# Four stages of a network kernel in another order: decay sums and levels, the out projection, grouped queries, the last rows

## The chip, the cores and the metric

The kernel runs on one core of a Trainium2 chip. The metric is the device time of one execution in microseconds (us). A core has five engines that work side by side: PE (TensorE: matmuls and transposes), DVE (VectorE), ACT (ScalarE), POOL (GpSimd) and SP, which issues most of the DMAs. Each takes its own instructions in order and waits on semaphores for the others. Matmul results land in PSUM, which this kernel uses as 8 banks of 128x512 float32; everything else lies in SBUF.

## The reference, cut to what matters

256 tokens of width 1024 go through a first block and a two-layer second block. In short:

```python
# first block, one layer
proj = rms_norm(x, l0_norm_mix) @ l0_w_in            # q (scaled), k, v, r, gate input
b = cumsum(log_sigmoid(gk_low @ w_gk_up + b_gk) / 16)
attn[i, j] = sum_k q[i, k] * k[j, k] * exp(b[i, k] - b[j, k])      # j <= i, 4 heads
x = x + (rms_norm(attn @ v) * silu(r)) @ l0_w_out
x = x + square(relu(rms_norm(x, l0_norm_ffn) @ l0_w_ff1)) @ l0_w_ff2
x = rms_norm(x, final_norm)
# second block, layer 0: neighbourhood attention and a gated feed-forward, latents and context
# second block, layer 1, latents only: grouped queries, 16 query heads on 4 key heads
q = axial_rope(rms_norm_2(q, q_gain));  k = axial_rope(rms_norm_2(k, k_gain))
s = einsum('bqhgd,bshd->bhgqs', q, concat([kc, k])) * dh ** -0.5
h = h + g1 * (softmax(s) @ concat([vc, v])) @ w_o
h = h + g2 * swiglu_ffn(ada_norm(h, norm_ffn[1]), ffn_w_in, ffn_w_out)
return rms_norm_2(h, norm_final_2)
```

## The kernel before, in words

**Precision and weights.** Every weight product is made of three passes (`mm3`, lines 177 to 180): weight and activation are each split into a rounded part and a remainder. A weight unit is a 128x1024 tile; `w_load` (L150) has SP load it into one of five raw buffers, `w_split` makes the rounded part on ACT (L161) and the remainder on DVE (L162). Both go into a pool of twelve buffers, so six units fit at most. `wnext` hands out the next unit of a fixed list, and `cap[0]` says how many units from the one handed out on are split ahead (3 means two more). For a token tile of 128, `mm_r` makes 6 matmuls of 128x512 (two halves of the output by three passes), `mm_h` 3.

**Order.** The tile framework plans the order on each engine from the program's order and from its own estimates of durations. Where `manual_schedule` is open, the named engines keep the order of the program: SP, ACT and DVE for the first products (lines 367 to 474), ACT alone until the gate products end (475 to 654), DVE and ACT at the very end (1509 to 1543). PE is planned everywhere.

**Decay sums and levels (lines 428 to 579).** Eight units give q and k, transposed (loop `f`). `decay_sums(t)` makes the cumulated log decay `bT` of a token tile: 4 matmuls (L431) and 2 ACT copies (L433); tile 0 at `f == 7`, tile 1 after the first unit (`k == 0`) of the next loop. That loop makes v from eight units; beside it `core_step` builds the 128x128 attention of both tiles by a diagonal, seven levels (distances 1 to 64) and the part across the tiles. The first part of a level makes subtractions on DVE (L501, L502), an exp on ACT (L504), products on DVE (L507, L508); its second part 16 small matmuls on PE (L522) and a masked copy on DVE (L528), for the two widest levels copies on ACT (L525, L516). `core_step` runs the second part of one unit and the first part of the next: one step of lead. `conditioning` (k == 2) starts loads of 1 MB, which wait for `bT` of tile 1.

**Out projection (lines 660 to 681).** Eight units of `l0_w_out`. Units 0 to 2 are multiplied with both token tiles at once; units 3 to 7 are kept (`late`), multiplied with tile 0, then with tile 1, so that `residual` of tile 0 (L658) and its transposes and splits (`to_T`: L217 on PE, L224 on ACT, L225 on DVE) lie beside the products of tile 1. `heads_T(range(4, 8))` (L630 on PE, L633, L634) stands after unit 2; all eight transposes of `to_T` stand before the last unit of tile 1.

**Grouped queries (lines 1245 to 1451).** Keys and values come first, `kv_finish` normalizes and rotates the keys and transposes them (L1237, L1241, L1243). Then the queries, in two halves of 8 heads by two token tiles, each of 8 steps of 3 matmuls. `q_proj(0)` makes half 0 for both tiles in turn, 16 steps, beside `kv_finish`; then a one-column Exp loads ACT's table (L1326); `q_finish` of half 0, tile 0 (L1274 to L1298) runs beside ten steps of half 1 (`q_proj1`). `staged` starts a head of a tile (`gqa_unit`) on each round: scores (L1387, L1388), maximum on DVE (L1393), exp on ACT (L1396), scaling (L1402 on DVE, L1400 on ACT), transposes (L1406), copies (L1413) and, for each four heads, the products with v (L1420). On each round `qfill` adds one of the six steps of half 1 that are left, steps of the other `q_finish` and of the out projection.

**Last rows (lines 1509 to 1543).** The last four units of the last down projection are kept back. For tile 1 three column pieces are made (512, 256, 256); each gets gate and residual (L1499, L1500) and its square sum on ACT (L1502). Then comes the root on POOL (L1538), ACT scales half 1 (L1539), DVE half 0 (L1541), and two DMAs write them.

Of the kernel before, what the change touches and what calls it, by code (L numbers as in the profile page):

```python
# [19 lines left out]
KD = D // P  # L20
# [63 lines left out]
def net(ctx, tc, x, xt, small, gk_up, gk_b, g_onorm, wst, final_norm, ctx_in, ctx_t, ada, ada_b, cvec,  # L84
# [122 lines left out]
    def to_T(*args):  # L207
        for _ in to_T_steps(*args):
            pass
# [226 lines left out]
    for f in range(8):  # L436
# [35 lines left out]
        if f == 7:  # L472
            decay_sums(0)
# [85 lines left out]


    vtok = []
    ac = [[bank() for _ in range(2)] for _ in range(NT)]
    for k in range(KD):
        u = wnext(("r", "w_in", k))
        for t in range(NT):
            mm_r(ac[t], u, xT[k], t, k == 0, k == KD - 1)
        if k == 0:
            decay_sums(1)
        if k == 2:
            conditioning()  # L570
        if k == 5:
            cap[0] = 3
        core_step()
# [88 lines left out]
    for k in range(KD):  # L662
        u = wnext(("r", "w_out", k))
        if k == 0:
            for t in range(NT):
                gated_heads(t, 1)
        if k < KD - 5:
            for t in range(NT):
                mm_r(ac[t], u, yT[k], t, k == 0, False)
        else:  # L670
            late.append((k, u))
    heads_T(range(4, KD))
    hT = new_T()
    for t in range(NT):
        for k, u in late:
            if (t, k) == (1, KD - 1):
                to_T([xin[0]], hT, 0, vc[:, V_FFN0, :])
            mm_r(ac[t], u, yT[k], t, False, k == KD - 1)
        residual(xin[t], ac[t])
    late.clear()  # L680
# [564 lines left out]
    def q_proj(hf, ac):  # L1245
        for kp in range(4):
            u = wnext(("h", "gqa_qkv", 2 * kp, 512 * hf))
            for j in range(2):
                k = 2 * kp + j
                for t in range(2):  # L1250
                    mm_h(ac[t], u, j, bT2[k], t, k == 0, k == KD - 1)
                    yield

    q1_units = []

    def q_proj1(ac, t):
        for kp in range(4):
            if t == 0:
                if kp == 2:
                    cap[0] = 0  # L1260
                q1_units.append(wnext(("h", "gqa_qkv", 2 * kp, 512)))
            for j in range(2):
                k = 2 * kp + j
                mm_h(ac[t], q1_units[kp], j, bT2[k], t, k == 0, k == KD - 1)
                yield
# [56 lines left out]
    aq = [bank(), bank()]  # L1322
    beside(q_proj(0, aq), back)
    run(back, 100)
    warm = col()
    A.activation(out=warm[:, 0:1], in_=aq[0][:, 0:1], func=AF.Exp, scale=0.0)  # L1326
    aq0, acq1 = [aq[0], t2([512])], aq[1]
    back = q_finish(0, aq0, 0)
    aq = [bank(), bank()]
    projs = [q_proj1(aq, t) for t in range(2)]  # L1330
    for n in range(10):
        run(projs[n // 8])
        run(back)
        if n == 1:
            A.copy(out=aq0[1], in_=acq1)
    run(back, 100)

    def finishes():

        yield from q_finish(1, aq, 0)  # L1340
        yield from q_finish(0, aq0, 1)
        run(projs[1], 9)
        q1_units.clear()
        yield from q_finish(1, aq, 1)
# [94 lines left out]
    def qfill(n):  # L1439
        run(projs[1])  # L1440
# [84 lines left out]
    ms, zs_ = col(), [t2([512]) for _ in range(2)]  # L1525
    for n, (hf, lo, w) in enumerate(((0, 0, 512), (1, 0, 256), (1, 256, 256))):
# [7 lines left out]
        if n > 0:  # L1534
            V.tensor_tensor(out=zs_[1][:, lo:lo + w], in0=zs_[1][:, lo:lo + w], in1=nfb[1][:, lo:lo + w], op=ALU.mult)
# [3 lines left out]
    A.activation(out=zs_[1], in_=zs_[1], func=AF.Copy, scale=r)  # L1539
    out_rows(nc.scalar, 1, 512, zs_[1])  # L1540
    V.scalar_tensor_tensor(out=zs_[0], in0=zs_[0], scalar=r, in1=nfb[0], op0=ALU.mult, op1=ALU.mult)  # L1541
    out_rows(nc.sync, 1, 0, zs_[0])
# [107 lines left out]
```

## Time and profile before

| what | value |
|---|---|
| time, median of 3 runs | 1268.24 us (1267.25 to 1268.48) |
| the profiled execution | 1267.33 us, of it the span of the profile 1265.5 us |
| PE busy | 1249.0 us, 99% of the span |
| DVE busy | 920.0 us, 73% |
| ACT busy | 686.1 us, 54% |
| granted PE clock | 0.998 |

The span runs from the first instruction to the last; 1.83 us of the time lie around it. A row of the timeline has start, length, engine, line, operation, tiles, and in brackets how long the engine was idle before it and what ended that. The records of matmuls overlap: one lasts longer than the time until the next one starts, so that PE's idle time is more than its rows show. PEld is the load of the stationary operand, in the shade of PE.

### The profile page before, as it was taken

The page shows a single profiled execution, that of the slowest core. Times are in us where ns is not written, and L with a number is a line of the kernel's source. Part 1 is how long each engine was busy: PE and PEld are TensorE (multiplying, and loading weights), DVE is VectorE, ACT ScalarE, POOL GpSimd, SP SyncE. Part 2 cuts the span into 40 slices and gives each one's busy share as a digit, 9 for nine tenths or more (in the row PEclk, how much of TensorE's full clock was granted, in tenths as well). Part 3 has the DMA queues.
Part 4 walks back from the last instruction along what each step waited for, and adds up shares of the span by engine and source line. Part 5 has one row for each costly group of instructions (what it writes and reads, how often), then busy time and mean ns, then how long its engine had stood idle before and what let it go on. Part 6 is the DMA issues. An engine that isn't in the chain of part 4 may idle for free.

```text
span 1265.5 us, 18648 instructions
## 1 busy us (share of the span) xinstructions
PE 1249.0 (99%) x6874; PEld 1043.6 (82%) x6874; DVE 920.0 (73%) x1629; ACT 686.1 (54%) x1335; POOL 79.2 (6%) x139
## 2 busy tenths in 40 slices
PE   9999999999999999999999999999999999999997
PEld 8878898988888777789888888888888677899996
DVE  5868788797988888777877667623668888655555
ACT  7565655666548888754332122323457797644443
POOL 1000000030100000001000000000002320000000
PEclk9999999999999999999999999999999999999999
DMA  8646587877572334463656777633664224665650
GB/s 302 202 133 212 190 293 255 283 267 260 183 251 98 126 114 114 155 197 114 210 184 204 248 258 252 219 100 102 198 200 117 67 84 128 215 190 184 187 180 34
DMA packets 68507, 231.22 MB, mean 183 GB/s; under 512 B 8048, under 2 KB 8736, under 8 KB 68416
## 3 DMA queue, kind: packets, MB, share of 16 engines
q1 hardware_dynamic: 68128, 229.68, 56.0%
q8 instruction: 54, 0.88, 0.3%
q10 hardware_dynamic: 288, 0.35, 0.1%
q14 instruction: 37, 0.30, 0.1%
HBM read 228.93 MB, written 1.07 MB: 182 GB/s over the span
## 4 chain that ended last, share of the span: by engine, by line
PE 84%; DVE 7%; ACT 6%; issue 1%; DMA 1%; POOL 0%; POOLq 0%; SPq 0%; DVEq 0%; ACTq 0%
PE b L178 26%; PE b L179 25%; PE b L180 25%; DVE wl L162 2%; PE b L1420 1%; ACT wh L161 1%; PE b L217 1%; PE b L1406 1%; PE b L522 1%; DMA raw<-in_wst_dram 1%; DVE a L309 1%; ACT t L878 1%; DVE t L309 1%; PE b L1387 0%; PE b L957 0%
## 5 line engine op out<-in xcount | busy, mean ns | idle before, releaser
L161 ACT CAST wh<-raw 128x1024 fp32r<-128x1024 f32 x310 | 322.8, 1044 | 391.2 <-PE b L179 295.7
L162 DVE TENSOR_TENSOR wl<-raw,wh 128x1024 fp32r<-128x1024 f32 x310 | 375.0, 1215 | 157.7 <-ACT wh L161 154.0
L179 PE MATMUL b<-t,wl 128*128 128x256 f32 (+1 forms) x1120 | 365.8, 327 | 0.3 <-DVE wl L162 0.3
L178 PE MATMUL b<-t,wh 128*128 128x256 f32 (+1 forms) x1120 | 366.1, 327 | 0.0
L180 PE MATMUL b<-t,wh 128*128 128x256 f32 (+1 forms) x1120 | 365.3, 327 | 0.0
L178 PE MATMUL b<-wh,t 128*128 128x512 f32 (+1 forms) x748 | 298.2, 401 | 1.2 <-ACT t L235 0.6
L180 PE MATMUL b<-wl,t 128*128 128x512 f32 (+1 forms) x748 | 295.1, 395 | 0.0
L179 PE MATMUL b<-wh,t 128*128 128x512 f32 (+1 forms) x748 | 294.9, 394 | 0.1
L179 PEld LDWEIGHTS b<-t,wl 128*128 128x128 f32 x1120 | 210.8, 188 | 22.6 <-DVE wl L162 0.6
L178 PEld LDWEIGHTS b<-t,wh 128*128 128x128 f32 x1120 | 210.7, 188 | 22.3 <-issue 0.2
L180 PEld LDWEIGHTS b<-t,wh 128*128 128x128 f32 x1120 | 210.5, 188 | 20.6 <-DVE t L236 0.2
L180 PEld LDWEIGHTS b<-wl,t 128*128 128x128 f32 x748 | 140.5, 188 | 33.7
L178 PEld LDWEIGHTS b<-wh,t 128*128 128x128 f32 x748 | 140.4, 188 | 32.6 <-ACT t L235 1.0
L179 PEld LDWEIGHTS b<-wh,t 128*128 128x128 f32 x748 | 140.8, 188 | 31.0 <-DVE t L634 0.6
L309 DVE CUSTOM_DVE_ANT_0 a<-a,crow 128x1024 f32<-128x1024 f32 x96 | 117.0, 1226 | 28.3 <-DMA a<-in_ada_dram 27.7
L309 DVE CUSTOM_DVE_ANT_0 t<-a,crow 128x1024 bf16<-128x1024 f32 x64 | 78.5, 1236 | 8.8 <-DMA a<-in_ada_dram 8.8
L1065 DVE TENSOR_TENSOR t<-b,t 128x512 f32<-128x512 f32 (+1 forms) x42 | 23.6, 563 | 59.4 <-PE b L180 52.2
L190 POOL TENSOR_TENSOR c<-c,mhalf 128x1 f32<-128x1 f32 x21 | 14.2, 674 | 537.7 <-DVE c L189 537.6
L324 POOL TENSOR_TENSOR mod<-mod,bcol 128x8 f32<-128x8 f32 x20 | 14.4, 719 | 478.3 <-DVE mod L309 476.0
L1071 ACT CAST t<-t 128x512 fp32r<-128x512 f32 (+1 forms) x42 | 21.7, 517 | 34.6 <-DVE t L1065 34.6
L197 ACT ACTIVATE t<-t 128x512 f32<-128x512 f32 x40 | 24.8, 624 | 10.8 <-DVE t L1034 6.4
L1396 ACT ACTIVATE t<-b,c,c 128x512 f32<-128x512 f32 x32 | 25.9, 811 | 3.4 <-POOL c L1394 3.4
(239 smaller groups left out, 1201.4 us busy)
## 6 DMA issues: line engine op xcount, KB each, us to landing
raw<-in_wst_dram SPq DMA_DIRECT2D x310, 512.0 KB, 4.4
a<-in_ada_dram SPq DMA_DIRECT2D x96, 512.0 KB, 4.4
t<-in_rpb_dram SPq DMA_DIRECT2D x16, 256.0 KB, 4.1
t<-row SPq DMA_DIRECT2D x12, 256.0 KB, 4.9
t<-in_ctx_dram SPq DMA_DIRECT2D x8, 256.0 KB, 5.8
t<-in_xt_dram SPq DMA_DIRECT2D x4, 256.0 KB, 5.9
t<-in_x_dram SPq DMA_DIRECT2D x4, 256.0 KB, 6.3
crow<-in_cvec_dram SPq DMA_DIRECT2D x2, 512.0 KB
```

The source lines that it names most:

```text
L161: A.copy(out=h[:, :n], in_=raw[:, :n])
L162: V.tensor_tensor(out=l[:, :n], in0=raw[:, :n], in1=h[:, :n], op=ALU.subtract)
L178: T.matmul(o, lhsT=lh, rhs=rh, start=first, stop=False)
L179: T.matmul(o, lhsT=ll, rhs=rh, start=False, stop=False)
L180: T.matmul(o, lhsT=lh, rhs=rl, start=False, stop=last)
L190: G.tensor_tensor(out=ms[:, 3:4], in0=ms[:, 2:3], in1=mhalf[:, 0:1], op=ALU.pow)
L197: A.activation(out=junk[hf], in_=halves[hf], func=AF.Square, scale=1.0 / 32.0, accum_out=ms[:, hf:hf + 1])
L309: V.tensor_tensor_reduce(out=raw if ci == n_c - 1 else t2([D], BF16), in0=raw, in1=crow[ci], scale=1.0, scalar=0.0, op0=ALU.mult, op1=ALU.add,
L324: G.tensor_tensor(out=m, in0=m, in1=bcol[:, L, v, :], op=ALU.add)
L1065: V.tensor_tensor(out=a, in0=pg_[:, :n], in1=a, op=ALU.mult)
L1071: A.copy(out=h, in_=a)
L1396: A.activation(out=pl, in_=sl, func=AF.Exp, scale=r, bias=mx[:, 1:2], accum_out=mx[:, 2:3])
```

## The change

Decay sums: tile 0 after `f == 6`, tile 1 after `f == 7`. Levels: two units (the diagonal, whose first part is empty, and the first level) are opened ahead of the loop, so that `core_step` opens a unit two steps before its matmuls. Out projection: four units are kept instead of five; the transposes of heads 4 and 5 stand after unit 1, those of 6 and 7 after unit 2; the steps of `to_T` for tile 0 stand 2, 3 and 3 ahead of the last three units of tile 1. Grouped queries: half 0 is made for tile 0 alone, then for tile 1 with its four units kept in SBUF; the table load and `q_finish` of tile 0 start after the first eight steps; only five steps of half 1 stand ahead of `staged`, and eleven are left for its rounds (two on each of the first two rounds, then one); `cap` is 2 there instead of 0. Last rows: the products with the final norm's gains go into tiles of their own, `ys_`, that of half 0 ahead of the root; the last operation on DVE becomes a scaling by one column.

```diff
@@ -469,8 +469,8 @@
         if f == 5:
             later_operands()
             cap[0] = 5
-        if f == 7:
-            decay_sums(0)
+        if f > 5:
+            decay_sums(f - 6)
     in_order.__exit__(None, None, None)
     in_order = tc.manual_schedule(engines={mybir.EngineType.Activation})
     in_order.__enter__()
@@ -557,6 +557,10 @@
             open_.append(core.pop(0))
             run(open_[-1])
 
+    for _ in range(2):
+        open_.append(core.pop(0))
+        run(open_[-1])
+
 
     vtok = []
     ac = [[bank() for _ in range(2)] for _ in range(NT)]
@@ -564,8 +568,6 @@
         u = wnext(("r", "w_in", k))
         for t in range(NT):
             mm_r(ac[t], u, xT[k], t, k == 0, k == KD - 1)
-        if k == 0:
-            decay_sums(1)
         if k == 2:
             conditioning()
         if k == 5:
@@ -664,19 +666,22 @@
         if k == 0:
             for t in range(NT):
                 gated_heads(t, 1)
-        if k < KD - 5:
+        if k < KD - 4:
             for t in range(NT):
                 mm_r(ac[t], u, yT[k], t, k == 0, False)
         else:
             late.append((k, u))
-    heads_T(range(4, KD))
+        if k in (1, 2):
+            heads_T((2 * k + 2, 2 * k + 3))
     hT = new_T()
+    first_T = to_T_steps([xin[0]], hT, 0, vc[:, V_FFN0, :])
     for t in range(NT):
         for k, u in late:
-            if (t, k) == (1, KD - 1):
-                to_T([xin[0]], hT, 0, vc[:, V_FFN0, :])
+            if t == 1 and k > KD - 4:
+                run(first_T, k - KD + 5)
             mm_r(ac[t], u, yT[k], t, False, k == KD - 1)
         residual(xin[t], ac[t])
+    run(first_T, KD)
     late.clear()
 
 
@@ -1242,26 +1247,14 @@
                 else:
                     V.tensor_copy(out=dst[h][:, pos:pos + P], in_=pt[:, h * P:(h + 1) * P])
 
-    def q_proj(hf, ac):
+    def q_proj(hf, t, units, o):
+
         for kp in range(4):
-            u = wnext(("h", "gqa_qkv", 2 * kp, 512 * hf))
+            if t == 0:
+                units.append(wnext(("h", "gqa_qkv", 2 * kp, 512 * hf)))
             for j in range(2):
                 k = 2 * kp + j
-                for t in range(2):
-                    mm_h(ac[t], u, j, bT2[k], t, k == 0, k == KD - 1)
-                    yield
-
-    q1_units = []
-
-    def q_proj1(ac, t):
-        for kp in range(4):
-            if t == 0:
-                if kp == 2:
-                    cap[0] = 0
-                q1_units.append(wnext(("h", "gqa_qkv", 2 * kp, 512)))
-            for j in range(2):
-                k = 2 * kp + j
-                mm_h(ac[t], q1_units[kp], j, bT2[k], t, k == 0, k == KD - 1)
+                mm_h(o, units[kp], j, bT2[k], t, k == 0, k == KD - 1)
                 yield
 
     qst, qf = {}, {}
@@ -1319,29 +1312,43 @@
     beside(kv_steps(acl), back)
     run(back, 100)
     back = alternate([kv_finish(acl, t) for t in range(2)])
-    aq = [bank(), bank()]
-    beside(q_proj(0, aq), back)
+    qu, aq = [[], []], [[bank(), None], [None, None]]
+    for _ in q_proj(0, 0, qu[0], aq[0][0]):
+        next(back, None)
+    warm = col()
+    A.activation(out=warm[:, 0:1], in_=aq[0][0][:, 0:1], func=AF.Exp, scale=0.0)
+    aq[0][1] = bank()
+    first = q_finish(0, aq[0], 0)
+    for _ in q_proj(0, 1, qu[0], aq[0][1]):
+        next(back, None)
+        next(first, None)
+    qu[0].clear()
+    q01 = t2([512])
+    A.copy(out=q01, in_=aq[0][1])
+    aq[0][1] = q01
+
+    def q1_products():
+        for t in range(2):
+            if t == 0:
+                cap[0] = 2
+            aq[1][t] = bank()
+            yield from q_proj(1, t, qu[1], aq[1][t])
+        qu[1].clear()
+
+    q1_ = q1_products()
+    for _ in range(5):
+        run(q1_)
+        next(back, None)
+        next(first, None)
     run(back, 100)
-    warm = col()
-    A.activation(out=warm[:, 0:1], in_=aq[0][:, 0:1], func=AF.Exp, scale=0.0)
-    aq0, acq1 = [aq[0], t2([512])], aq[1]
-    back = q_finish(0, aq0, 0)
-    aq = [bank(), bank()]
-    projs = [q_proj1(aq, t) for t in range(2)]
-    for n in range(10):
-        run(projs[n // 8])
-        run(back)
-        if n == 1:
-            A.copy(out=aq0[1], in_=acq1)
-    run(back, 100)
+    run(first, 100)
 
     def finishes():
 
-        yield from q_finish(1, aq, 0)
-        yield from q_finish(0, aq0, 1)
-        run(projs[1], 9)
-        q1_units.clear()
-        yield from q_finish(1, aq, 1)
+        yield from q_finish(1, aq[1], 0)
+        yield from q_finish(0, aq[0], 1)
+        run(q1_, 20)
+        yield from q_finish(1, aq[1], 1)
 
     def oproj():
 
@@ -1437,7 +1444,7 @@
     gorder = [(h, t) for t in range(2) for h in range(16)]
 
     def qfill(n):
-        run(projs[1])
+        run(q1_, 2 if n < 2 else 1)
         run(finish_, 0 if n < 3 else 2 if n < 8 or n % 4 == 0 else 1)
         run(oproj_)
 
@@ -1522,7 +1529,7 @@
         out_rows(nc.sync, 0, 512 * hf, z0[hf])
 
 
-    ms, zs_ = col(), [t2([512]) for _ in range(2)]
+    ms, zs_, ys_ = col(), [t2([512]) for _ in range(2)], [t2([512]) for _ in range(2)]
     for n, (hf, lo, w) in enumerate(((0, 0, 512), (1, 0, 256), (1, 256, 256))):
         o = bank()[:, 0:w] if n else ac[1][0]
         last_mms(o, 1, 512 * hf + lo, w, n > 0)
@@ -1531,15 +1538,15 @@
             V.scalar_tensor_tensor(out=ms[:, 3:4], in0=ms[:, 0:1], scalar=EPS, in1=ms[:, 1:2], op0=ALU.add, op1=ALU.add)
         else:
             first_rows(n)
-        if n > 0:
-            V.tensor_tensor(out=zs_[1][:, lo:lo + w], in0=zs_[1][:, lo:lo + w], in1=nfb[1][:, lo:lo + w], op=ALU.mult)
+        for y, z, g in ((ys_[1][:, lo:lo + w], zs_[1][:, lo:lo + w], nfb[1][:, lo:lo + w]), (ys_[0], zs_[0], nfb[0]))[:(0, 2, 1)[n]]:
+            V.tensor_tensor(out=y, in0=z, in1=g, op=ALU.mult)
     V.tensor_tensor(out=ms[:, 2:3], in0=ms[:, 2:3], in1=ms[:, 3:4], op=ALU.add)
     r = ms[:, 4:5]
     G.tensor_tensor(out=r, in0=ms[:, 2:3], in1=mhalf[:, 0:1], op=ALU.pow)
-    A.activation(out=zs_[1], in_=zs_[1], func=AF.Copy, scale=r)
-    out_rows(nc.scalar, 1, 512, zs_[1])
-    V.scalar_tensor_tensor(out=zs_[0], in0=zs_[0], scalar=r, in1=nfb[0], op0=ALU.mult, op1=ALU.mult)
-    out_rows(nc.sync, 1, 0, zs_[0])
+    A.activation(out=ys_[1], in_=ys_[1], func=AF.Copy, scale=r)
+    out_rows(nc.scalar, 1, 512, ys_[1])
+    V.tensor_scalar(out=ys_[0], in0=ys_[0], scalar1=r, scalar2=None, op0=ALU.mult)
+    out_rows(nc.sync, 1, 0, ys_[0])
     in_order.__exit__(None, None, None)
```

## The prediction

> **What bounds the kernel now.** I read the page first, then PE's list of waits, the windows, and the timeline where PE waits.
>
> ```profile
> span 1265.5 us, 18648 instructions
> PE 1249.0 (99%) x6874; PEld 1043.6 (82%) x6874; DVE 920.0 (73%) x1629; ACT 686.1 (54%) x1335; POOL 79.2 (6%) x139
> ```
> ```profile
> PE b L522 <- DVE t L508: 1.6, 1, 1.6
> ...
> PE b L1406 <- DVE t L1402: 1.1, 3, 0.5
> PE b L1406 <- DVE c L1398: 0.8, 2, 0.5
> ...
> PE b L217 <- DVE t L225: 0.4, 1, 0.4
> ...
> PE b L179 <- DVE wl L162: 0.3, 1, 0.3
> ```
>
> PE is busy for 99% of the span, and no edit takes a matmul away. So the change can only win what PE waits, or shorten the work after its last matmul. The listed waits are what it aims at: the levels (L522), the start of grouped queries (L1406), the out projection (L217, a weight at L179).
>
> A wait costs more than its row says:
>
> ```profile
> 969.42 0.39 PE L178 MATMUL b<-wh,t 128*128 128x512 f32 x1
> 969.65 0.39 PE L179 MATMUL b<-wh,t 128*128 128x512 f32 x1
> ```
> ```profile
> 112.97 0.48 PE L178 MATMUL b<-wh,t 128*128 128x512 f32 x1
> 113.30 0.40 PE L179 MATMUL b<-wh,t 128*128 128x512 f32 x1
> ```
>
> Matmuls start 0.23 us apart but are shown 0.39 long, so 0.16 of each wait lies under the record before it; I add 0.16 per wait. The second pair stands right behind a group of transposes: its gap is 0.33 instead of 0.23. So each change from transposes to weight products costs about 0.1, and an edit that breaks a group up pays that again.
>
> ```profile
> core 0: us, PE busy (x) PEld busy (x) DVE busy (x) ACT busy (x) POOL busy (x), PEclk, DMA share, GB/s
> 37.00:44.40 7.40, 7.40 (x46) 6.49 (x45) 3.70 (x4) 3.75 (x7) 0.42 (x3) 1.00 0.90 341
> 44.40:72.00 27.60, 26.05 (x156) 22.40 (x155) 27.19 (x64) 11.34 (x16) 0.00 (x0) 1.00 0.36 115
> 965.20:986.00 20.80, 20.80 (x105) 16.96 (x103) 16.29 (x41) 13.15 (x30) 5.35 (x6) 1.00 0.58 175
> 986.00:992.50 6.50, 6.24 (x30) 4.80 (x28) 4.68 (x9) 4.62 (x9) 2.63 (x4) 1.00 0.26 81
> 992.50:1006.40 13.90, 11.65 (x70) 7.53 (x70) 12.80 (x31) 12.23 (x33) 4.60 (x11) 1.00 0.14 39
> ```
>
> In two of these stretches DVE, not PE, sets the pace: 27.19 of 27.60 us in the levels, 12.80 of 13.90 where grouped queries start. The stretch ahead of each has DVE at 50% and 78%. Work that starts earlier fits in there.
>
> **Decay sums and levels.**
>
> ```profile
> 38.16 1.05 PE L431 MATMUL b<-cm,t 128*128 128x128 f32 x8
> ...
> 39.26 0.65 ACT L433 COPY t<-b 128x256 f32<-128x256 f32 x2 [1.38 <-PE b L431]
> ...
> 44.45 0.42 DVE L501 TENSOR_TENSOR t<-t 128x256 f32<-128x256 f32 x1
> ```
> ```profile
> 64.09 1.34 DVE L528 COPY_PREDICATED t<-masks,b 128x512 f32<-128x512 uint8 x2
> ...
> 71.28 2.02 PE L522 MATMUL b<-t 128*128 128x128 f32 x16 [1.55 <-DVE t L508]
> 71.39 0.42 DVE L508 TENSOR_TENSOR t<-t,t 128x256 f32<-128x256 f32 x1
> ```
>
> Six levels take DVE from 44.45 to 71.81, 27.4 us; PE catches up at the sixth and waits 1.55 + 0.16 = 1.71. In the new order L431 of tile 1 moves ahead of 12 products (12 x 0.23 = 2.8 us), and the first level opens at once instead of a step later: the copies of L433 end at 39.26 + 0.65 - 2.8 = 37.1, and DVE can begin. In front of the sixth level it then has the same 27.4, the 3.7 that it did from 37.0 to 44.4, and two pairs of masked copies less (L528, 2.7), since those of the fourth and fifth level now come behind: it ends at 37.1 + 27.4 + 3.7 - 2.7 = 65.5. PE asks for the sixth level one step (2.8) earlier, at 71.28 - 1.71 - 2.8 = 66.8. So the stall goes whole or down to a few tenths, against 1.71 now; PE has weight products left to plan in between. ACT keeps the program's order there, so the weight casts queue behind two exps that wait for DVE; `cap` 5 has four units split ahead, which covers it, and without that cover it costs the 1.7 us of four subtractions (4 x 0.42). The 1 MB that POOL releases from `bT` comes up to 2.8 us earlier into a window with the DMAs at 0.90; the same four units cover that, and at 341 GB/s its whole price would be 3 us. I take **-1.6**; ends 0 and -1.8.
>
> **Out projection.**
>
> ```profile
> 128.64 0.58 PE L217 MATMUL b<-cm,t 128*128 128x128 f32 x2 [0.37 <-DVE t L225]
> ```
>
> The eight transposes of tile 0 stand in one block and wait for their banks behind L225: 0.37 + 0.16. Spread by 2, 3 and 3 over products of 1.4 us (6 x 0.23) each, a group of three needs three L225 in that time, and the block's wait goes. The late weight (0.3 + 0.16) goes too: with four kept units instead of five, the last unit is asked for 6 matmuls, 1.4 us, later. Against it stand two more changes between transposes and products, 0.2. The transposes of heads 4 and 5 come a unit earlier and may wait for the gated heads; the plan has unit 2 to put in front. Sum 0.53 + 0.46 - 0.2 = 0.8, **-0.8**; ends +0.3 (nothing but the breaks) and -1.2.
>
> **Grouped queries.**
>
> ```profile
> 965.21 0.40 PE L178 MATMUL b<-wh,t 128*128 128x512 f32 x1
> ...
> 967.03 1.23 DVE L162 TENSOR_TENSOR wl<-raw,wh 128x1024 fp32r<-128x1024 f32 x1 [0.24 <-ACT wh L161]
> ...
> 976.88 0.39 PE L180 MATMUL b<-wl,t 128*128 128x512 f32 x1
> ```
> ```profile
> 986.17 0.50 PE L1387 MATMUL b<-t,t 128*128 128x512 f32 x1
> ...
> 992.72 0.63 PE L1406 MATMUL b<-cm,t 128*128 128x128 f32 x4 [0.47 <-DVE t L1402]
> ```
> ```profile
> 1006.39 0.50 PE L178 MATMUL b<-wh,t 128*128 128x512 f32 x1 [0.27 <-ACT t L1413]
> ```
>
> From 992.72 to 1006.39 PE has used up the six filler steps and waits seven times; the two rows are the first and the last of them. The windows give 0.26 + 2.25 = 2.5 us without PE, and with 7 x 0.16 it is 3.6. The change leaves five more steps, 15 matmuls, 5 x 0.70 = 3.5 us, for these rounds. The stall shrinks by that only if the rounds, DVE's pace included, also start 3.5 earlier, at 986.17 - 3.5 = 982.7. Two conditions. The first queries: half 0 of tile 0 ends 8 steps after 965.21, at 970.8, and before it took 986.17 - 976.88 = 9.3 from the last product of half 0 to the first score, so 980.1; met with 2.6 to spare, the table load moving along on ACT. DVE: its 16.29 + 4.68 + 12.80 = 33.8 us from 965.2 to 1006.4 must fit in 37.7, 90%, just under the 92% of the dense stretch. I take off five breaks of 0.1 and 0.2 for the tightness: **-2.8**; ends +1 (DVE late for the first scores by one split of 1.2, filler no help) and -3.6. The split of the out projection's first unit, which `cap` 2 moves ahead of the rounds, is in the 33.8 already.
>
> **Last rows.**
>
> ```profile
> 1257.30 0.28 PE L180 MATMUL b<-wl,t 128*128 128x256 f32 x1
> ```
> ```profile
> 1258.03 0.42 DVE L1535 TENSOR_TENSOR t<-t,t 128x256 f32<-128x256 f32 x1 [0.97 <-ACT t L1502]
> 1258.38 0.41 DVE L1499 TENSOR_TENSOR t<-b,t 128x256 f32<-128x256 f32 x1
> ...
> 1259.61 0.19 ACT L1502 ACTIVATION_READ_ACCUMULATOR t<-t 128x1 f32 x1
> 1259.83 0.42 DVE L1535 TENSOR_TENSOR t<-t,t 128x256 f32<-128x256 f32 x1 [0.51 <-ACT t L1502]
> 1260.17 0.15 DVE L1536 TENSOR_TENSOR c<-c 128x1 f32<-128x1 f32 x1
> ...
> 1261.04 0.72 ACT L1539 ACTIVATE t<-t,c 128x512 f32<-128x512 f32 x1 [1.25 <-POOL c L1538]
> ```
>
> L1535 writes in place and waits for ACT's square, 0.97 and 0.51. With `ys_` it needn't: the first begins at 1257.06, and the added product of 512 columns (two of 256, 0.7) follows; DVE is free at 1258.1, after PE's end, so L1499 gains 0.28. The second no longer stands in front of L1536, which then follows the accumulator's read, 1259.61 - 0.28 + 0.19 = 1259.52, at 1259.57 instead of 1260.17. DVE's last operation gets shorter, but ACT's 0.72 beside it ends last. **-0.6**; ends -0.3 and -0.9.
>
> **Sum:** 1.6 + 0.8 + 2.8 + 0.6 = 5.8. The profiled execution took 1267.33, so 1261.5; it lies 0.9 under the median of the runs, and from 1268.24 the forecast is **1262.4**.
>
> **A rule against it.** Granted PEclk is 1.00 even from 992.5 to 1006.4, where PE is busy for 11.65 of 13.90 us. The Trainium skill, Perfetto Trace Analysis, section Matmul Optimizations, says that the engine scales power with use, so "it's important that matmuls execute back-to-back in batches". By that rule, breaking up transposes and fillers could lower the clock. The row shows no such drop in a far looser stretch.
>
> **Rivals.** (1) DVE holds the start of grouped queries: for it speak 92% in the dense stretch, against it the 78% ahead of it. That term becomes 0 to -0.6: 1265.0. Chance 0.22. (2) The planner does not follow: PE's order is its own, and it hoisted filler before; out projection and queries then give nothing, 1268.24 - 2.2 = 1266.0. Chance 0.09. (3) Slower: a weight unit for one tile lasts only 6 matmuls, 1.40 us, and its split costs 1.04 on ACT and 1.22 on DVE.
>
> ```profile
> L161 ACT CAST wh<-raw 128x1024 fp32r<-128x1024 f32 x310 | 322.8, 1044 | 391.2 <-PE b L179 295.7
> L162 DVE TENSOR_TENSOR wl<-raw,wh 128x1024 fp32r<-128x1024 f32 x310 | 375.0, 1215 | 157.7 <-ACT wh L161 154.0
> ```
>
> If splits stop running ahead, because the kept units fill the twelve buffers, each of the eight takes 2.26 instead of 1.40: +6.9, and the queries' gain is lost: 1268.24 - 3.0 + 6.9 = 1272.1. It decides once a split ends more than 1.40 after the one before. Against it: the last split of half 0 ended at 968.3 and would be asked for at 965.21 + 3 x 1.40 = 969.4. Chance 0.07. (4) The clock: one of PE's loose stretches, such as the 13.9 us, if the clock fell by half there, would cost up to 13.9: 1276. Chance 0.01. (5) More is won, as later waits of the rounds move too: 1259. Chance 0.06.
>
> The forecast keeps 0.55. The range 1259.4 to 1266.8 leaves out (3), (4), part of (5) and the far ends of (1) and (2), under 0.2. A difference under 0.2%, 2.5 us, can't be told from none: the line lies at 1265.7. Faster: 0.55 + 0.06 + 0.16 of (1) + 0.03 of (2) = 0.80; slower 0.08; same 0.12.
>
> **What would show it.** Levels: no wait of L522 for L508, L501 from about 37. Out projection: no wait at L217. Queries: first score near 979 (982.7 less the gains before it), weight products between the first L1406 groups, DVE over 85% ahead of them. Last rows: no wait of the two products for L1502, the root 0.6 sooner after PE's end. Wrong if PE waits for L162 in the query halves, or if the L1406 waits still add to 2 us or more.

## The result and the profile after

The changed kernel takes 1260.24 us (median of 5 executions, 1259.76 to 1261.04); the kernel before took 1267.59 beside it (5 executions, 1267.24 to 1268.48). The ratio is 0.9943, with a 95% interval of 0.9929 to 0.9957: faster, by 7.35 us. The forecast was 1262.4, worked out from 1268.24; of the 2.2 us between, 0.65 is that the kernel before itself has a lower median with two more executions.

The profiled execution after took 1259.76, its span is 1258.0. Its page:

```profile
span 1258.0 us, 18656 instructions
PE 1246.1 (99%) x6874; PEld 1043.5 (83%) x6874; DVE 920.0 (73%) x1630; ACT 685.8 (55%) x1335; POOL 80.8 (6%) x139
```

PE does the same 6874 matmuls in a shorter span and DVE one instruction more. PE's list of waits, which was headed by L522:

```profile
PE b L121 <- POOL mhalf L137: 1.3, 1, 1.3
PE b L178 <- ACT t L235: 0.6, 1, 0.6
PE b L179 <- DVE wl L162: 0.5, 1, 0.5
PE b L1413 <- DVE t L1409: 0.4, 1, 0.4
...
PE b L1413 <- ACT t L1407: 0.4, 1, 0.4
```

L522 and L217 are gone. L1413, which was L1406, keeps two waits; the third row is still there and will matter below. (Against the kernel before, the lines of the changed kernel stand 5 higher from L669 on, 7 lower in `q_finish`, L1262 to L1292, and 7 higher from L1330 on.) The windows after, those of grouped queries cut at the same landmarks as before, in us, with busy time and number of PE, PEld, DVE, ACT and POOL, then PEclk, DMA share and GB/s:

```profile
37.00:44.40 7.40, 7.40 (x44) 6.40 (x44) 6.62 (x16) 4.20 (x6) 0.84 (x3) 1.00 0.87 331
44.40:70.00 25.60, 25.60 (x159) 22.59 (x158) 25.60 (x57) 11.33 (x16) 0.00 (x0) 1.00 0.38 114
961.57:978.90 17.33, 17.33 (x91) 14.25 (x90) 14.44 (x38) 12.13 (x30) 5.65 (x6) 1.00 0.44 146
978.90:985.40 6.50, 6.50 (x30) 5.22 (x29) 5.97 (x14) 4.35 (x8) 2.61 (x4) 1.00 0.56 164
985.40:999.64 14.24, 13.85 (x83) 10.00 (x81) 13.26 (x29) 12.96 (x33) 4.63 (x11) 1.00 0.27 75
```

DVE did 3.70 us in the 7.4 ahead of the levels and does 6.62; PE has no hole left in the levels. In the three rows of grouped queries DVE has 33.67 us of work in 38.07, 88%, and the rounds that held PE to 11.65 of 13.90 us now hold it to 13.85 of 14.24. The granted clock is 1.00 in all of them.

Where the time went, by stage: each number is how much a stage's last landmark moved against before, less what the stages ahead had already brought (start times from the two timelines; negative is earlier). Beside it are the four runs that make one part of the change alone.

| stage, up to | after | levels alone | out projection alone | queries alone | last rows alone |
|---|---|---|---|---|---|
| levels, first product of the heads | -1.89 | -2.06 | +0.06 | +0.10 | +0.09 |
| out projection, first transpose of the feed-forward | -1.32 | -0.34 | -1.34 | -0.35 | -0.26 |
| neighbourhood attention and feed-forward, first key transpose | -0.42 | +0.15 | -0.39 | -0.42 | -0.46 |
| grouped queries, last of their products | -2.85 | +0.05 | +0.01 | -2.89 | +0.03 |
| last feed-forward, last matmul | -0.07 | -0.07 | +0.88 | +0.88 | -0.09 |
| last operations, end | -1.01 | +0.01 | +0.01 | 0.00 | -1.00 |
| sum | -7.56 | -2.26 | -0.77 | -2.68 | -1.69 |

The diagonal holds the parts, and they do not disturb one another. Three entries off it repeat where nothing was edited: 0.3 in the out projection, 0.4 behind it, and 0.9 in the last feed-forward; they are taken up at their places.

### The profile page after: what moved, and what is told of

It reads as the page before. It is cut to its first block, busy times and chain, and to the rows that moved or that the text cites. A ratio compares the mean times of both kernels' runs of the same rounds, so it can differ in the third digit from the quotient of the medians.

```text
span 1258.0 us, 18656 instructions
## 1 busy us (share of the span) xinstructions
PE 1246.1 (99%) x6874; PEld 1043.5 (83%) x6874; DVE 920.0 (73%) x1630; ACT 685.8 (55%) x1335; POOL 80.8 (6%) x139
## 4 chain that ended last, share of the span: by engine, by line
PE 87%; ACT 6%; DVE 5%; issue 1%; DMA 0%; POOL 0%; POOLq 0%; ACTq 0%
PE b L178 26%; PE b L179 26%; PE b L180 26%; DVE wl L162 1%; PE b L1427 1%; PE b L217 1%; PE b L1413 1%; ACT wh L161 1%; PE b L522 1%; ACT t L883 1%; PE b L1394 1%; ACT t L905 0%; PE b L962 0%; DVE a L309 0%; DVE t L309 0%
## 5 line engine op out<-in xcount | busy, mean ns | idle before, releaser
L161 ACT CAST wh<-raw 128x1024 fp32r<-128x1024 f32 x310 | 322.7, 1045 | 391.5 <-PE b L179 283.7
L162 DVE TENSOR_TENSOR wl<-raw,wh 128x1024 fp32r<-128x1024 f32 x310 | 374.6, 1215 | 154.2 <-ACT wh L161 151.6
L179 PE MATMUL b<-t,wl 128*128 128x256 f32 (+1 forms) x1120 | 365.7, 327 | 0.5 <-DVE wl L162 0.5
L179 PE MATMUL b<-wh,t 128*128 128x512 f32 (+1 forms) x748 | 294.7, 394 | 0.0
L179 PEld LDWEIGHTS b<-t,wl 128*128 128x128 f32 x1120 | 210.9, 188 | 22.8 <-DVE wl L162 0.7
L179 PEld LDWEIGHTS b<-wh,t 128*128 128x128 f32 x748 | 140.9, 188 | 30.2 <-DVE t L236 0.5
L309 DVE CUSTOM_DVE_ANT_0 a<-a,crow 128x1024 f32<-128x1024 f32 x96 | 117.1, 1227 | 27.7 <-DMA a<-in_ada_dram 27.2
L309 DVE CUSTOM_DVE_ANT_0 t<-a,crow 128x1024 bf16<-128x1024 f32 x64 | 78.6, 1237 | 8.6 <-DMA a<-in_ada_dram 8.5
```

The lines of the kernel that those rows point to most:

```text
L161: A.copy(out=h[:, :n], in_=raw[:, :n])
L162: V.tensor_tensor(out=l[:, :n], in0=raw[:, :n], in1=h[:, :n], op=ALU.subtract)
L179: T.matmul(o, lhsT=ll, rhs=rh, start=False, stop=False)
L309: V.tensor_tensor_reduce(out=raw if ci == n_c - 1 else t2([D], BF16), in0=raw, in1=crow[ci], scale=1.0, scalar=0.0, op0=ALU.mult, op1=ALU.add,
```

## The experiments: each part alone

Four kernels are the kernel before with one part of the change.

**Levels alone.**

```diff
-        if f == 7:
-            decay_sums(0)
+        if f > 5:
+            decay_sums(f - 6)
...
+    for _ in range(2):
+        open_.append(core.pop(0))
+        run(open_[-1])
...
-        if k == 0:
-            decay_sums(1)
```

> The kernel before with the decay sums and levels of the change alone. Theory (the four parts add up, each in its own stage): the heads' first products with v come 1.9 us earlier than before, as in the changed kernel, no wait of L522 for L508, and every later landmark moves by the same 1.9; span about 1263.6. Rival (the parts need each other through the planner's order): 1 us or less, or given back by the out projection, whose weight at L179 and transposes would wait longer when PE arrives earlier.

Measured: 1265.05 us median, ratio 0.9982 (0.9973 to 0.9992), levels 2.06 sooner, no wait at L522.

**Out projection alone.**

```diff
-        if k < KD - 5:
+        if k < KD - 4:
...
-    heads_T(range(4, KD))
+        if k in (1, 2):
+            heads_T((2 * k + 2, 2 * k + 3))
...
-            if (t, k) == (1, KD - 1):
-                to_T([xin[0]], hT, 0, vc[:, V_FFN0, :])
+            if t == 1 and k > KD - 4:
+                run(first_T, k - KD + 5)
```

> The kernel before with the out projection of the change alone. Theory: up to the heads' products nothing moves; from there to the feed-forward's first transposes (tok_T) 1.3 us less, no wait of the transposes of tile 0 for L225; span about 1264.2. Rival (the out projection only gained because it starts earlier against the weights' DMAs): 0.5 us or less.

Measured: 1266.55 us in one execution, beside a median of 1267.47 before. The stage is 1.34 sooner and the wait at L217 is gone; 0.88 of it is lost again in the last feed-forward, which has no edit.

**Queries alone**, all hunks of that stage; their core:

```diff
-    beside(q_proj(0, aq), back)
+    for _ in q_proj(0, 0, qu[0], aq[0][0]):
+        next(back, None)
...
-    for n in range(10):
-        run(projs[n // 8])
-        run(back)
...
+    for _ in range(5):
+        run(q1_)
+        next(back, None)
+        next(first, None)
```

> The kernel before with the grouped queries of the change alone. Theory: from the keys' first transposes to the last product with v 2.85 us less, as in the changed kernel; nothing else moves; span about 1262.6. Rival (the stage profits from a changed phase of the weights' loads): under 2 us.

Measured: 1264.59 us median, ratio 0.9978 (0.9969 to 0.9988). The stage is 2.89 sooner.

**Last rows alone**, the hunks with `ys_`:

```diff
-    ms, zs_ = col(), [t2([512]) for _ in range(2)]
+    ms, zs_, ys_ = col(), [t2([512]) for _ in range(2)], [t2([512]) for _ in range(2)]
...
-    V.scalar_tensor_tensor(out=zs_[0], in0=zs_[0], scalar=r, in1=nfb[0], op0=ALU.mult, op1=ALU.mult)
+    V.tensor_scalar(out=ys_[0], in0=ys_[0], scalar1=r, scalar2=None, op0=ALU.mult)
```

> The kernel before with the last rows of the change alone. Theory: nothing moves up to PE's last matmul; from there to the last operation 0.76 us less, to the end of the span 1.0 us less; span about 1264.5. Rival (DMAs of the outputs set the end): last operation 0.76 earlier, the end under 0.5.

Measured: 1265.63 us in one execution, beside 1267.47. From the last matmul to the last operation 0.75 less, to the end 1.00 less.

## The experiments: why each part works

These start from the changed kernel and take back one thing.

**Levels: the earlier sums, or the two units opened ahead?** The sums stay early, the two units are not opened:

```diff
-    for _ in range(2):
-        open_.append(core.pop(0))
-        run(open_[-1])
-
```

> The changed kernel without the two units opened ahead: the decay sums stay early, a level has one step of lead again. Theory of the prediction (DVE must begin its levels at 37 instead of 44): with the first level opened behind two casts it begins 2 us or more late, and L522 waits again, 0.5 to 1.7 us. Rival (the early decay sums alone do it, since the planner may hoist DVE's work): no wait, heads' products as in the changed kernel within 0.2.

1262.81 us in one execution. The levels' whole gain is lost, 1.96; the timeline of this kernel shows where:

```profile
37.56 0.65 ACT L433 COPY t<-b 128x256 f32<-128x256 f32 x2
...
42.99 0.69 DVE L490 TENSOR_TENSOR t<-b,cm 128x512 f32<-128x512 f32 x1 [2.57 <-PE b L488]
...
44.49 0.42 DVE L501 TENSOR_TENSOR t<-t 128x256 f32<-128x256 f32 x1
...
71.33 2.02 PE L522 MATMUL b<-t 128*128 128x128 f32 x16 [1.55 <-DVE t L508]
```

The sums are copied by 38.2, and yet DVE begins the levels at 44.49, as before, and PE waits the same 1.55 at the same place. Without the lead the first level comes behind the diagonal, and DVE first waits 2.57 for the diagonal's matmuls (L488) whose result it multiplies by the identity (L490). The changed kernel:

```profile
36.55 0.65 ACT L433 COPY t<-b 128x256 f32<-128x256 f32 x2 [0.52 <-PE b L431]
36.95 0.43 DVE L501 TENSOR_TENSOR t<-t 128x256 f32<-128x256 f32 x1 [0.44 <-ACT t L433]
...
66.15 0.42 DVE L508 TENSOR_TENSOR t<-t,t 128x256 f32<-128x256 f32 x1
...
66.69 1.95 PE L522 MATMUL b<-t 128*128 128x128 f32 x16
```

So the two units opened ahead are what wins. The program needs the early sums for them, since L501 reads `bT`, but alone the early sums win nothing. (1.1 us more were lost in this execution in neighbourhood attention, which has no edit: a wait of 0.9 at L893, which two other runs show with 0.3 and 0.5 and the rest not at all.)

**Out projection: the block of transposes.** The eight transposes for the feed-forward again in one block:

```diff
-            if t == 1 and k > KD - 4:
-                run(first_T, k - KD + 5)
+            if (t, k) == (1, KD - 1):
+                run(first_T, KD)
```

> The changed kernel with all eight transposes of token tile 0 ahead of the last unit again; four kept units and early transposes of the heads stay. Theory (spreading pays): a wait of the transposes for L225 of 0.3 to 0.5 us shown, 0.7 to 1.0 us longer to the feed-forward's first transposes. Rival (one kept unit less pays, by the weights): 0.3 us or less longer.

1262.3 us in one execution; the stage is 0.96 later, and 0.97 more went in the last feed-forward. The timeline of this kernel, and behind it that of the changed one:

```profile
126.46 0.58 PE L217 MATMUL b<-cm,t 128*128 128x128 f32 x2 [0.37 <-DVE t L225]
```
```profile
120.99 0.38 PE L217 MATMUL b<-cm,t 128*128 128x128 f32 x2
122.61 0.49 PE L217 MATMUL b<-cm,t 128*128 128x128 f32 x3
124.33 0.49 PE L217 MATMUL b<-cm,t 128*128 128x128 f32 x3
```

The planner runs six of the eight transposes, then six products, then the two that wait. The wait of 0.37 shown is 0.54 between starts. Behind it the second transpose comes after 0.26 instead of 0.11, and from there to the second product it is 0.59 instead of 0.35. That is 0.93 of the 0.96. In groups of 2, 3 and 3 none of it appears, although there is one group more. With the block the stage is still 0.37 ahead of the kernel before, hardly more than the 0.26 to 0.35 of the runs without an edit there: one kept unit less and earlier transposes of the heads show no gain of their own beside that.

**Queries: filler, or an earlier finish?** Ten steps ahead of the rounds, as before, the first half still one tile at a time:

```diff
-    for _ in range(5):
+    for _ in range(10):
```

> The changed kernel with ten steps of the second query half ahead of the rounds, as many as before, instead of five. Theory (the filler pays): the waits of the probabilities' transposes come back, 2.5 us or more shown, and from the keys' transposes to the last product with v it takes 2.0 to 2.9 us longer than in the changed kernel. Rival (the first queries' earlier finish pays, by spreading DVE's work): under 1 us longer.

1262.7 us in one execution; the stage is 2.89 later, all that it had won, and the waits of the rounds are back:

```profile
991.49 0.63 PE L1413 MATMUL b<-cm,t 128*128 128x128 f32 x4 [1.27 <-ACT t L1277]
992.88 0.63 PE L1413 MATMUL b<-cm,t 128*128 128x128 f32 x4 [0.30 <-DVE t L1409]
...
996.46 0.63 PE L1413 MATMUL b<-cm,t 128*128 128x128 f32 x4 [0.50 <-DVE c L1405]
```

The transposes of the first queries came at the same time as in the changed kernel. Queries that are finished earlier win nothing by themselves, and neither does the `cap` of 2, which this kernel has too; the time is won by the steps kept for the rounds.

**The other half of that: five steps, but both tiles in turn.** The kernel before, its second half's products in one generator, five steps ahead and the rest left to the rounds as in the changed kernel (L1391 is L1387 of before):

```diff
-    projs = [q_proj1(aq, t) for t in range(2)]
-    for n in range(10):
-        run(projs[n // 8])
+    def both():
+        for t in range(2):
+            yield from q_proj1(aq, t)
+
+    q1_ = both()
+    for n in range(5):
+        run(q1_)
...
-        run(projs[1])
+        run(q1_, 2 if n < 2 else 1)
```

> The kernel before with one thing changed: five steps of the second half's products ahead of the rounds instead of ten, the first half still with both tiles in turn. It tells what taking one tile at a time contributes. Theory (both parts are needed): half 0 ends for both tiles together at about 976.9, the first queries cannot be ready for their transposes before about 982, only 3.5 us of products stand in between, so PE waits some 1.5 to 4 us ahead of the first score, and of the 2.9 that the grouped queries gained 0 to 1.5 are left, or it is slower than the kernel before. Rival (the filler alone does it): first score at about 982.4, no wait ahead of it, and the whole 2.9 from the first key and value transposes to the last product of the rounds.

1265.56 us in one execution, beside 1268.29. The stage is 0.95 sooner, a third of 2.85. Neither theory had the way right: PE waits only 0.33 ahead of the first score. The timeline of this kernel:

```profile
977.75 0.47 PE L178 MATMUL b<-wh,t 128*128 128x512 f32 x1
...
983.64 0.85 PE L1294 MATMUL b<-identr,t 128*128 128x128 f32 x8
...
984.83 0.50 PE L1391 MATMUL b<-t,t 128*128 128x512 f32 x1 [0.33 <-ACT t L1298]
```

From 977.75 to 983.64 PE runs 24 weight products: eight steps, not five. The planner puts three of the kept steps in front of the first queries' transposes, which come at 983.6. Eight are left for the rounds, two more than before. Up to the fourth group of products with v this kernel is 1.72 ahead of the kernel before; in that group it loses 0.76 by another order on PE, which the next run shows, and 0.95 is left. So taking one tile at a time is what frees the other three steps: the first queries' transposes come 18.0 us behind the first key transpose instead of 21.9, while half 0 of the other tile is still being multiplied. Of the 2.85 it is worth 1.1 by the state ahead of that group and 1.9 in all. This kernel also keeps `cap` at 0 in that place; whether that has a part in it was not tested.

**Still fewer ahead.** The changed kernel with three steps instead of five:

```diff
-    for _ in range(5):
+    for _ in range(3):
```

> The new kernel with three steps of weight products ahead of the rounds instead of five, so that eight are left as filler (ten steps ahead had cost 2.9 us, all of what the grouped queries had gained). Filler theory: what PE still waits in the rounds after five steps is 0.52 at 995.6, 0.43 at 999.9 and 0.62 at 1049.4 of the first score's stage; two steps more (1.4 us) can cover the first two, so the last product of the rounds comes 0.5 to 0.9 us sooner. Rival, the first queries' transposes are late: they stood at 976.5 with five steps and with ten, and if DVE and ACT are what they wait for, two steps less ahead only move 1.4 us of waiting in front of the first score, and the last product of the rounds comes at the same time or up to 0.5 later.

1261.83 us in one execution; the stage is 0.39 longer than in the changed kernel. That is the rival's size, but not its way: no wait moves in front of the first score, which starts 0.9 sooner in the stage. As the filler theory had it, the first of the waits that are left in the rounds goes (0.52 between starts), and up to the fourth group of products with v this kernel is 0.38 ahead. It loses 0.76 inside that group. This kernel first, then the changed one:

```profile
1022.89 0.65 PE L1427 MATMUL b<-t,t 128*64 128x256 f32 x2
1023.47 0.51 PE L1394 MATMUL b<-t,t 128*128 128x512 f32 x1
1023.90 1.94 PE L1427 MATMUL b<-t,t 128*64 128x256 f32 x14
1025.78 0.50 PE L1395 MATMUL b<-t,t 128*128 128x512 f32 x1
```
```profile
1022.50 1.95 PE L1427 MATMUL b<-t,t 128*64 128x256 f32 x16
```

The planner puts the first matmul of a score between the products. In the changed kernel the sixteen products start in eight pairs, the two of a pair 0.007 us apart; here four of them start alone, and from the transposes ahead of the group to those behind it, with the same work in between, it takes 3.42 us instead of 2.66. The run with both tiles in turn has the same break and the same 3.42. So of ten, five and three, five is best as the planner orders them (2.89, 0 and 0.39 more), but that three steps ahead are too few is not shown.

**Last rows: the product that was added.** The product of half 0 goes back into DVE's last operation:

```diff
-        for y, z, g in ((ys_[1][:, lo:lo + w], zs_[1][:, lo:lo + w], nfb[1][:, lo:lo + w]), (ys_[0], zs_[0], nfb[0]))[:(0, 2, 1)[n]]:
+        for y, z, g in ((ys_[1][:, lo:lo + w], zs_[1][:, lo:lo + w], nfb[1][:, lo:lo + w]), (ys_[0], zs_[0], nfb[0]))[:(0, 1, 1)[n]]:
...
-    V.tensor_scalar(out=ys_[0], in0=ys_[0], scalar1=r, scalar2=None, op0=ALU.mult)
+    V.scalar_tensor_tensor(out=ys_[0], in0=zs_[0], scalar=r, in1=nfb[0], op0=ALU.mult, op1=ALU.mult)
```

> The changed kernel with the product of half 0 and its gain back in the last operation of DVE. Theory (ACT's 0.72 beside it ends last, the wait for the squares was all): the root comes at the same time, last operation up to 0.03 later, the end of the span 0 to 0.1 later. Rival (the earlier issue of one of the two output DMAs is worth something): the end 0.2 to 0.3 later.

1259.74 us in one execution, and neither theory had it: the tail gets shorter. The tail of the changed kernel first, then that of the same edit run again for the timing further down:

```profile
1250.54 1.03 DVE L1542 TENSOR_TENSOR t<-t,t 128x256 f32<-128x256 f32 x2
...
1250.74 0.28 PE L180 MATMUL b<-wl,t 128*128 128x256 f32 x1
...
1251.49 0.42 DVE L1506 TENSOR_TENSOR t<-b,t 128x256 f32<-128x256 f32 x1
...
1252.94 0.16 DVE L1543 TENSOR_TENSOR c<-c 128x1 f32<-128x1 f32 x1
1253.18 0.54 POOL L1545 TENSOR_TENSOR c<-c,mhalf 128x1 f32<-128x1 f32 x1 [4.21 <-DVE c L1543]
1253.75 0.72 ACT L1546 ACTIVATE t<-t,c 128x512 f32<-128x512 f32 x1 [0.85 <-POOL c L1545]
1253.76 0.49 DVE L1548 TENSOR_SCALAR t<-t,c 128x512 f32<-128x512 f32 x1 [0.66 <-POOL c L1545]
```
```profile
1250.83 0.28 PE L180 MATMUL b<-wl,t 128*128 128x256 f32 x1
...
1251.15 0.42 DVE L1506 TENSOR_TENSOR t<-b,t 128x256 f32<-128x256 f32 x1
...
1253.42 0.72 ACT L1546 ACTIVATE t<-t,c 128x512 f32<-128x512 f32 x1 [0.85 <-POOL c L1545]
1253.42 0.75 DVE L1548 SCALAR_TENSOR_TENSOR t<-t,c,t 128x512 f32<-128x512 f32 x1 [0.66 <-POOL c L1545]
```

In the changed kernel L1542 runs twice, and L1506 starts 0.75 behind the start of PE's last matmul; with one product it starts 0.32 behind it. The 0.43 stays on the path, and the last operation ends 0.39 sooner after PE's end without the early product. At the end 0.2 of it is left: in the changed kernel the two closing transfers are issued 0.24 apart (DVE's 0.49 ends sooner than ACT's 0.72), and the end comes 3.5 behind the last operation; issued 0.03 apart, 3.7.

**The product in POOL's time.** The same product on DVE no longer ahead of the last subtraction but behind the add of the sums, where DVE has nothing to do (so L1546 is the root, L1545 of the changed kernel):

```diff
-        for y, z, g in ((ys_[1][:, lo:lo + w], zs_[1][:, lo:lo + w], nfb[1][:, lo:lo + w]), (ys_[0], zs_[0], nfb[0]))[:(0, 2, 1)[n]]:
+        for y, z, g in ((ys_[1][:, lo:lo + w], zs_[1][:, lo:lo + w], nfb[1][:, lo:lo + w]), (ys_[0], zs_[0], nfb[0]))[:(0, 1, 1)[n]]:
...
+    V.tensor_tensor(out=ys_[0], in0=zs_[0], in1=nfb[0], op=ALU.mult)
     r = ms[:, 4:5]
     G.tensor_tensor(out=r, in0=ms[:, 2:3], in1=mhalf[:, 0:1], op=ALU.pow)
```

> The new kernel with the added product of half 0 moved on DVE from in front of the last subtraction to behind the add of the sums, where DVE has nothing to do while POOL takes the root. Theory (the product in front of the last subtraction costs what it delays it): from PE's last matmul to the last compute 0.4 us less than in the new kernel, as where the product had been put back into DVE's last operation (3.06 there, 3.45 in the new kernel); here the last operation stays short as well, 0.49 instead of 0.75, so about 0.4 to 0.5 less, and the end 0.2 to 0.5 sooner. Rival, the product in the hole delays the last operation instead: 0.69 of product from 0.2 behind the add ends just when POOL's 0.54 does, so half 0 could end 0.2 later and the output's transfer with it: end no sooner than in the new kernel.

1260.56 us in one execution. The tail is hardly shorter than in the changed kernel, 3.42 to the last operation against 3.45, but not for the rival's reason:

```profile
1253.43 0.16 DVE L1543 TENSOR_TENSOR c<-c 128x1 f32<-128x1 f32 x1
1253.51 0.68 DVE L1544 TENSOR_TENSOR t<-t,t 128x512 f32<-128x512 f32 x1
1253.67 0.93 POOL L1546 TENSOR_TENSOR c<-c,mhalf 128x1 f32<-128x1 f32 x1 [3.78 <-DVE c L1543]
1254.63 0.72 ACT L1547 ACTIVATE t<-t,c 128x512 f32<-128x512 f32 x1 [1.23 <-POOL c L1546]
```

POOL's root takes 0.93 instead of 0.54 while DVE multiplies beside it, and ACT starts 1.20 behind the add instead of 0.81. That takes back what the earlier L1506 had won.

**The shortest tail, timed.** The product back in the last operation, in several executions:

> The new kernel with the product of half 0 back in DVE's last operation, timed this time, since it had the shortest end of all versions. If the 0.39 that it saved between PE's last matmul and the last compute belongs to the order of DVE's work, the tail is 3.05 to 3.10 again (3.45 in the new kernel) and the median of several executions lies 0.2 to 0.4 under that of the new kernel, 1259.8 to 1260.1, where the last feed-forward runs at the same spacing; that is too little for the totals to tell from the new kernel, and the ratio to the kernel before should be 0.9940 or 0.9941. Rival: the tail varies by 0.4 from execution to execution, then it is 3.4 or so here, and nothing is left.

1260.28 us median (1259.60 to 1260.50, 5 executions), ratio to the kernel before 0.9941 (0.9927 to 0.9954). Its tail is 3.07, as in the first run of that edit, so the 0.38 belongs to the order and not to one execution. The median that was expected, 1259.8 to 1260.1, did not come: in the whole this kernel cannot be told from the changed kernel's 1260.24; a gain of 0.2 lies inside the spread of 0.9 to 1.3 that either kernel has.

## Why the prediction was right, and where it was not

**Levels: right, a little small.** It said DVE starts at 37.1, PE asks for the sixth level at 66.8, and nothing waits; it was 36.95 and 66.69, and the 1.71 went whole. Taken 1.6, measured 1.89 and 2.06. It was a near thing, though: DVE's last product for that level ended at 66.57, where 65.5 was worked out, so 0.1 us ahead of PE and not 1.3. That ACT or the transfers would take some of it back did not show: no wait for L161 or L162 came up there.

**Out projection: near in the whole, wrong in each of its three terms.** The late weight was a misread row. "PE b L179 <- DVE wl L162: 0.3" is a wait at 8.5 us, long ahead of this stage, and stands in the profile after with 0.5; I had joined it to a gap of 0.29 at L179 at 118.95. What ended that gap is shown by the load of the stationary operand, in the profile before:

```profile
118.48 0.75 DVE L634 TENSOR_TENSOR t<-b,t 128x256 fp32r<-128x256 f32 x2
...
118.95 0.19 PEld L179 LDWEIGHTS b<-wh,t 128*128 128x128 f32 x1 [0.57 <-DVE t L634]
```

It is the remainder of the heads' transposes that came late, not a weight; on DVE a split (L162) stood ahead of it until 118.56. The gap is in the profiled execution of before alone: three runs with the same code there do not have it, and come 0.26 to 0.35 sooner by themselves (the table's second row). In the changed kernel the last L634 ends at 112.3, and no product waits for it. Second, the block of transposes costs 0.96, not 0.53, because smaller gaps follow the first one. Third, a change from transposes to products costs nothing, so the 0.2 for more breaks didn't come. The group ahead of the prediction's second pair of rows:

```profile
112.18 1.03 PE L630 MATMUL b<-cm,t 128*128 128x128 f32 x8
```

Eight transposes, 0.11 apart, put the first product at 113.06 and the second 0.23 later at 113.29; the second stands at 113.30. The first is shown 0.08 too soon, at 112.97, and that alone made the gap of 0.33. So about 1.0 belongs to the edit, where the sum had 0.8, and that the two are so close is luck.

**Grouped queries: right, the last tenths by luck.** First score at 979.09 where 979 was said, DVE at 88% where 90% was worked out, 2.85 won where 2.8 was taken. The 3.5 less 0.5 for breaks and 0.2 for tightness was not how it went: the breaks cost nothing, and two of the seven waits are left instead, 0.52 and 0.43 between starts:

```profile
995.57 0.55 PE L1413 MATMUL b<-cm,t 128*128 128x128 f32 x3 [0.36 <-ACT t L1407]
...
999.88 0.51 PE L178 MATMUL b<-wh,t 128*128 128x512 f32 x1 [0.27 <-ACT t L1420]
```

Both conditions are shown as conditions: without the filler nothing is left (ten ahead), without the early first queries a third (both tiles in turn; 1.72 ahead of the broken group). What was missed is that the planner itself moves filler in front where the queries are late.

**Last rows: mechanism right, price wrong.** L1506 stands nearer to PE's end, as said, by 0.33 (1.08 behind the last matmul before, 0.75 now). But it let L1506 stand behind the added product, "DVE is free at 1258.1, after PE's end", without a price for that, and this alone gives away 0.43. It was also said that DVE's shorter last operation changes nothing, since ACT's ends last; the transfers staggered by it give 0.25 at the end. Together 1.0 where 0.6 was taken.

**The rivals.** DVE holding the start of grouped queries, and a planner that does not follow, fall with the -2.85. Splits that do not run ahead fall too: the profile after shows no wait of PE for L162 or L161 in the stage. More was won than forecast, but by the terms above and not by later waits of the rounds. The clock stayed at 1.00 in every window shown; here the rule of the Trainium skill, Perfetto Trace Analysis, section Matmul Optimizations, that matmuls should run "back-to-back in batches", found nothing to decide. What broken batches cost in time was nothing at a change from transposes to products, and 0.76 us where a score stood between paired products.

**What is in no term.** The sum of the terms was 5.8, the profiled executions differ by 7.56: levels 0.3, out projection 0.5 (0.3 of it the gap of the execution before), last rows 0.4, 0.1 from grouped queries and the last feed-forward, and 0.4 from the stages between, where four runs without an edit there moved by +0.15 to -0.46; what moves them stays open.

## What to carry to other kernels

Where PE waits in rounds that alternate with another engine's work, filler in the rounds is worth what it covers of the waits (here 2.9 us for 3.5 us of products), but only if whatever had been using it as cover can do without: make the first results ready earlier, then keep the filler. A block of small operations that waits for its buffers is better spread between long ones; the wait is larger than its row, and the spreading cost nothing here. Before a wait is put into a sum, find its time on the timeline; the same two lines can wait for each other anywhere in the program, and what PE waited for may stand in the row of the operand's load. And when an edit moves work, look at the order that the planner makes of it: one score between paired products cost more than two steps of filler won.

## What the runs showed of the hardware

**POOL's root beside DVE.** The 0.93 is not by chance. In the profile after, one group of the same root elsewhere takes 0.54 to 0.57 in 18 of its 21 rows and 1.45 or 1.46 in three, and in each of the three DVE has just started an operation with two inputs in SBUF, such as:

```profile
309.66 1.22 DVE L162 TENSOR_TENSOR wl<-raw,wh 128x1024 fp32r<-128x1024 f32 x1
309.82 1.45 POOL L190 TENSOR_TENSOR c<-c,mhalf 128x1 f32<-128x1 f32 x1 [41.35 <-DVE c L189]
```

(One of the three stands beside L309, with two inputs as well.) POOL ends 0.39 behind DVE's end here (311.27 against 310.88) and 0.41 in the tail above (1254.60 against 1254.19): it does not finish until DVE is done. Beside L1506, which reads one input from PSUM, it took 0.54 (at 1248.43). The Trainium skill, SBUF — State Buffer, section Who interferes with whom, states that a VectorE instruction with two SBUF inputs contends with a GpSimd instruction that reads SBUF, and that the second to come blocks until the first is done; the rows agree.

**Two spacings of the same matmuls.** In the last feed-forward, which no run edited, PE is busy without a break at clock 1.00, and yet the same 140 us hold different numbers of the same matmuls. The windows of the changed kernel and of the out projection alone:

```profile
1100.00:1240.00 140.00, 140.00 (x1006) 131.37 (x1005) 72.67 (x83) 60.51 (x82) 0.00 (x0) 1.00 0.55 169
```
```profile
1100.00:1240.00 140.00, 140.00 (x997) 131.40 (x996) 72.68 (x83) 61.40 (x83) 0.00 (x0) 1.00 0.58 176
```

From start to start those of 256 columns take 117.3 ns in the one and 118.6 in the other, those of 512 columns 234.9 and 233.1. The profiled executions have either the one or the other, and the second makes the stage 0.9 to 1.0 us longer: out projection alone, queries alone, the block of transposes, three steps ahead and the product in POOL's time have it, the others not. No part of the change goes with it. What sets it stays open.
